# Norm weights and identity loaded on ACT's queue, and 18 matmuls on a zeroed tile ahead of the first input

## The chip, the core and the metric

The kernel runs on one core of a Trainium2 chip. The core has five engines that run side by side: TensorE (PE, matrix multiply), VectorE (DVE), ScalarE (ACT), GpSimd (POOL) and SyncE (SP). SP, ACT and POOL can issue DMA transfers. The metric is the device time of one execution in microseconds, median of several.

## The reference

One inference step of a two-layer encoder for 1024 prompt frames and 8 x 16 sample frames, that is 1152 tokens of width 1024 in all, in float32. Cut to what matters here, layer 0 begins so:

```python
xn = _rmsnorm(x, norm_g)                    # x * rsqrt(mean(x*x) + 1e-6) * norm_g
z = jnp.einsum('btd,de->bte', xn, w_in)     # 1024 -> 3584 columns
q, k, v, g_a, u_b, v_b, g_b = jnp.split(z, L0_SPLITS, axis=-1)
```

Differential attention and a spatial gate follow, an output projection, then layer 1 (a convolution module), and a last norm. The change touches only the first norm's weights `norm_g`, the identity matrix that the transposes use, and what PE does before its first input.

## The kernel before, in words

The 1152 tokens are 9 tiles of 128. For each tile `phase_qkv` loads `x` (128 x 1024, 512 KB), normalises it (`norm_transpose`), transposes it on PE in 8 blocks of 128 x 128 (`transpose_split`) and splits the result into a high part `xh` (a cast on ACT, L167) and a low part `xl` (a subtraction on DVE, L168). Matrix products are made of three products of such halves (`mm3`, L155): high by high, high by low, low by high. The weights are split the same way by `split_w`: a chunk `raw` of 512 KB is loaded by SP (L137), cast to `wh` on ACT (L143), and the remainder `wl` made on DVE (L144). One weight block of 512 columns has four such chunks, and each chunk serves two of the eight steps of a product. Three `raw` buffers exist, so the fourth chunk is loaded once the first has been split. `x` has two buffers, so tile 2 is loaded once tile 0 has been normalised.

Tile 0 is normalised in halves (`norm_out`): two sums of squares on ACT (L187), their sum on DVE (L188), a scale and offset (L123), a power on POOL (L124, `rr`), and two multiplications by `rr` and the norm weights `gb` on DVE (L193). `gb` holds `norm_g` in all 128 partitions, which one broadcast DMA fills (L114). The first product after that is the value projection, 24 matmuls of 512 columns per token tile, then keys and queries.

Each engine works through its own list in order. Those lists are written by a scheduler that reorders what the source says, so an edit at the top can change the order of casts on ACT and DVE. DMAs issued by one engine are queued in the order of issue.

## Time and profile before

| | us |
|---|---|
| median of 3 runs | 1261.32 |
| lowest and highest of these | 1260.91, 1264.07 |
| the profiled execution's own time | 1257.52 |
| its span, first to last instruction | 1255.7 |
| PE busy in the span | 1186.4 (94%) |
| PE's share of the chain that ended last | 77% |

PE is busy through nearly all of the span, so what counts is when its stream of work starts in earnest and where it stops. The table's PE time is no measure of PE's speed: matmuls overlap, and at the lower of the two clocks that the trace shows each one takes longer. In the timeline each row is a start, a duration, an engine, a line of the kernel, the operation, and in brackets how long the engine sat idle before it and what released it. In the chain of waits each row is a start, a duration and what held the end at that moment.

### The profile page before, as it was taken

How to read it: one execution, taken by the hardware profiler on the slowest of the kernel's cores; microseconds unless marked ns; L12 is line 12 of the kernel's file. 1: busy time of each engine (PE TensorE's matmuls, PEld its weight loads, DVE VectorE, ACT ScalarE, POOL GpSimd, SP SyncE). 2: the span in 40 equal slices, each digit the busy share in tenths (PEclk: the TensorE clock that was granted, in tenths of full speed). 3: DMA queues.
4: the chain of work that ended last, by engine and by line, in shares of the span. 5: the costliest groups of instructions: out<-in, count | busy, mean ns of one | idle time of the engine just before them, and what ended most of it. 6: DMA issues, size and time to landing. Idle time of an engine off the chain costs nothing.

```text
span 1255.7 us, 18564 instructions
## 1 busy us (share of the span) xinstructions
PE 1186.4 (94%) x6644; PEld 1078.1 (86%) x6644; DVE 830.0 (66%) x1695; ACT 477.6 (38%) x1090; POOL 365.6 (29%) x540
## 2 busy tenths in 40 slices
PE   6999999999989997889999999999999987999997
PEld 5878998999989887778888878999999987997886
DVE  5420225788687878686666535799999999267843
ACT  4431223445454545574544434211121212156421
POOL 2223223435353426222222221211424220033200
PEclk9999999999989999899999999999999997999999
DMA  8352444414141315685666545213231310212222
GB/s 295 106 164 70 152 150 128 119 55 116 39 124 42 112 41 163 225 287 203 223 213 232 185 150 184 66 40 88 72 108 49 122 59 24 67 35 101 101 96 73
DMA packets 121924, 153.26 MB, mean 122 GB/s; under 512 B 13577, under 2 KB 85281, under 8 KB 121824
## 3 DMA queue, kind: packets, MB, share of 16 engines
q1 hardware_dynamic: 107848, 108.21, 27.9%
q0 software_dynamic: 13840, 43.60, 10.2%
q8 instruction: 53, 0.87, 0.3%
q14 instruction: 39, 0.32, 0.1%
q10 hardware_dynamic: 144, 0.26, 0.1%
HBM read 116.22 MB, written 36.26 MB: 121 GB/s over the span
## 4 chain that ended last, share of the span: by engine, by line
PE 77%; DMA 8%; DVE 6%; ACT 4%; issue 2%; POOL 2%; SPq 0%; DVEq 0%; POOLq 0%; ACTq 0%
PE mm L155 50%; PE out L155 8%; PE py L1175 3%; PE S L155 3%; PE pa L589 2%; PE tr L416 2%; DMA vraw<-in_cache_v 2%; PE tr L165 2%; PE S L546 1%; PE S L547 1%; PE mm L787 1%; PE mm L761 1%; PE mm L786 1%; PE tr L584 1%; DVE wl L144 1%
## 5 line engine op out<-in xcount | busy, mean ns | idle before, releaser
L155 PE MATMUL mm<-yh,wh 128*128 128x384 f32 x576 | 196.5, 341 | 15.1 <-ACT sg L1024 12.6
L155 PE MATMUL mm<-yl,wh 128*128 128x384 f32 x576 | 195.2, 339 | 0.0
L155 PE MATMUL mm<-yh,wl 128*128 128x384 f32 x576 | 194.8, 339 | 0.0
L155 PE MATMUL mm<-wh,xh 128*128 128x384 f32 (+1 forms) x504 | 185.4, 369 | 1.3 <-DVE sg L469 0.6
L155 PE MATMUL mm<-wl,xh 128*128 128x384 f32 (+1 forms) x504 | 184.3, 366 | 1.7 <-DVE wl L144 1.7
L1151 DVE SCALAR_TENSOR_TENSOR acc<-u,cc,acc 128x1024 f32<-128x1024 f32 x145 | 185.4, 1279 | 0.4
L155 PE MATMUL mm<-wh,xl 128*128 128x384 f32 (+1 forms) x504 | 183.5, 364 | 0.0
L144 DVE TENSOR_TENSOR wl<-raw,wh 128x1024 fp32r<-128x1024 f32 (+1 forms) x72 | 91.3, 1274 | 91.6 <-ACT wh L143 91.0
L155 PEld LDWEIGHTS mm<-yh,wh 128*128 128x128 f32 x576 | 109.0, 189 | 15.9 <-ACT sg L1024 12.9
L155 PEld LDWEIGHTS mm<-yl,wh 128*128 128x128 f32 x576 | 109.1, 189 | 0.3
L155 PEld LDWEIGHTS mm<-yh,wl 128*128 128x128 f32 x576 | 109.0, 189 | 0.1
L155 PEld LDWEIGHTS mm<-wh,xh 128*128 128x128 f32 x504 | 95.5, 190 | 12.6 <-issue 1.1
L155 PEld LDWEIGHTS mm<-wl,xh 128*128 128x128 f32 x504 | 95.7, 190 | 11.7 <-DVE wl L144 3.2
L155 PEld LDWEIGHTS mm<-wh,xl 128*128 128x128 f32 x504 | 95.5, 190 | 8.8 <-DVE xl L168 0.3
L143 ACT CAST wh<-raw 128x1024 fp32r<-128x1024 f32 (+1 forms) x72 | 71.6, 1003 | 68.3 <-PE mm L155 30.6
L124 POOL TENSOR_TENSOR rr<-pw,mhalf 128x1 f32<-128x1 f32 x59 | 34.6, 586 | 169.2 <-DVE pw L123 160.8
L560 ACT ACTIVATE e<-S,nm 128x512 f32<-128x512 f32 (+5 forms) x96 | 55.2, 579 | 49.8 <-DVE nm L555 34.5
L1169 POOL TENSOR_TENSOR tw<-wx,same 128x640 f32<-128x640 f32 x24 | 37.4, 1560 | 80.3 <-PE py L1175 70.9
L552 DVE TENSOR_REDUCE nm<-S 128x1 f32<-128x512 f32 (+5 forms) x96 | 52.4, 550 | 12.1 <-PE S L547 11.4
L155 PE MATMUL out<-wh,cl 128*128 128x512 f32 x144 | 59.7, 415 | 0.0
L155 PE MATMUL out<-wh,ch 128*128 128x512 f32 x144 | 57.7, 401 | 1.7 <-DVE xr L847 1.2
L155 PE MATMUL mm<-wl,ch 128*128 128x512 f32 x144 | 56.9, 395 | 2.3 <-DVE wl L144 2.2
(287 smaller groups left out, 2572.7 us busy)
## 6 DMA issues: line engine op xcount, KB each, us to landing
raw<-in_cache_k SPq DMA_DIRECT2D x32, 512.0 KB, 4.5
vraw<-in_cache_v POOLq DMA_DIRECT2D x32, 512.0 KB, 5.2
raw<-in_w_in SPq DMA_DIRECT2D x24, 512.0 KB, 5.1
raw<-in_w_out SPq DMA_DIRECT2D x16, 512.0 KB, 4.1
raw<-in_w_in SPq DMA_DIRECT2D x32, 256.0 KB, 3.6
raw<-in_w_in SPq DMA_DIRECT2D x48, 128.0 KB, 3.2
s_y<-xr POOLq DMA_DIRECT2D x9, 512.0 KB, 5.5
x<-s_y SPq DMA_DIRECT2D x9, 512.0 KB, 4.1
```

What stands on the lines that cost most here:

```text
L124: m = nc.gpsimd.tensor_tensor(out, v[:, :w], self.mhalf[:, :w], ALU.pow)
L143: nc.scalar.copy(h[:, :ks * n], raw[:, :ks * n])
L144: (low or nc.vector).tensor_tensor(l[:, :ks * n], raw[:, :ks * n], h[:, :ks * n].bitcast(F32), ALU.subtract)
L155: m = self.nc.tensor.matmul(out, lhsT=x, rhs=y, start=(i == 0), stop=(i == n - 1))
L165: nc.tensor.transpose(ps[:, k * P:(k + 1) * P], src[:, kk * P:(kk + 1) * P], self.ident)
L416: nc.tensor.transpose(ps[:, h * P:(h + 1) * P], src[:, h * P:(h + 1) * P], self.ident)
L552: nc.vector.tensor_reduce(nm[:, j:j + 1], s[:, :n], AX.X, ALU.max, negate=True)
L560: nc.scalar.activation(e[:, j * n:(j + 1) * n], S[j][:, :n], AF.Exp, bias=nv, accum_out=zz[:, j:j + 1])
L589: nc.tensor.matmul(po, lhsT=wT[:, k * P:(k + 1) * P], rhs=hd["v"][:, k, :], start=(k == 0), stop=(k == qb))
L1151: tap = nc.vector.scalar_tensor_tensor(cv[:, :T] if k == CONV - 1 else acc, u[:, k:k + T], w1, acc, ALU.mult, ALU.add)
L1169: nc.gpsimd.tensor_tensor(tw.rearrange("p s (c f) -> p s c f", f=8), wx[:, g, :].rearrange("p (s f) -> p s f", f=8).unsqueeze(2).broadcast ...
L1175: nc.tensor.matmul(py, lhsT=tw[:, 4 - s, :], rhs=X[:, g, s:s + 176], start=(s == 0), stop=(s == 4))
```

## The change

Before the first token tile is loaded, a tile `warm` of 128 x 384 is zeroed on DVE, and PE multiplies two 128 x 128 pieces of it 18 times into a buffer that nothing reads. `gb` is loaded in two halves of 512 columns (256 KB each) from ACT's queue instead of in one piece from SP's, and the identity also goes to ACT's queue. `warm` takes a turn in the rotation of the `qh` buffers and the product a turn of the `pg` buffers.

```diff
+WARM = 18
...
+            warm = wk.tile([P, 384], F32, name="qh")
+            nc.vector.memset(warm, 0.0)
+            pw_ = pg.tile([P, 512], F32, name="pg")
+            for i in range(WARM):
+                nc.tensor.matmul(pw_[:, i % 4 * P:(i % 4 + 1) * P], lhsT=warm[:, :P], rhs=warm[:, P:2 * P], start=True, stop=True)
+            g0 = a["norm_g0"].partition_broadcast(P)
             for t in range(NT):
                 x = self.stage.tile([P, D], F32, name="x")
                 if t == 0:
                     for i in range(2):
                         nc.sync.dma_start(out=x[:, i * 512:(i + 1) * 512], in_=self.xrow(t)[:, i * 512:(i + 1) * 512])
+                        nc.scalar.dma_start(out=self.gb[:, i * 512:(i + 1) * 512], in_=g0[:, i * 512:(i + 1) * 512])
                 else:
                     nc.sync.dma_start(out=x, in_=self.xrow(t))
                 if t == 0:
-                    self.bcast(self.gb, a["norm_g0"])
-                    nc.sync.dma_start(out=self.ident, in_=a["cst"][:, :P])
+                    nc.scalar.dma_start(out=self.ident, in_=a["cst"][:, :P])
                 self.norm_transpose(x, self.gb, t)
```

The scheduler moves some casts. ACT's list at the start of the program before the change (`xs` with `x` alone is a sum of squares, `cst_58` the identity):

```order
L187 ACT_TABLE_LOAD
L187 ACTIVATE xs,ss_118<-x 128x512 x2
L143 CAST wh<-raw 128x1024
L167 CAST xh_82<-tr 128x4x128
L167 CAST xh_83<-tr 128x4x128
L143 CAST wh<-raw 128x1024 x2
L173 ACTIVATE xs,ss<-x 128x1024 x2
```

and ACT's list there with the change, where line numbers below the new constant are higher by one:

```order
L379 DMA gb<-in_norm_g 128x512 x2
L383 DMA cst_58<-in_cst 128x128
L188 ACT_TABLE_LOAD
L188 ACTIVATE xs,ss_140<-x 128x512 x2
L144 CAST wh<-raw 128x1024 x2
L168 CAST xh_82<-tr 128x4x128
L144 CAST wh<-raw 128x1024
L168 CAST xh_83<-tr 128x4x128
L174 ACTIVATE xs,ss<-x 128x1024 x2
```

Three DMA issues now stand ahead of everything on ACT, and the cast of the second weight chunk stands ahead of the first cast of the transposed tile. DVE's list at the same place before the change:

```order
L193 SCALAR_TENSOR_TENSOR xs<-x,rr,gb 128x512 x2
L144 TENSOR_TENSOR wl<-raw,wh 128x1024
L168 TENSOR_TENSOR xl_84<-tr,xh_82 128x4x128
L168 TENSOR_TENSOR xl_85<-tr,xh_83 128x4x128
L144 TENSOR_TENSOR wl<-raw,wh 128x1024 x2
```

and with the change:

```order
L194 SCALAR_TENSOR_TENSOR xs<-x,rr,gb 128x512 x2
L145 TENSOR_TENSOR wl<-raw,wh 128x1024 x2
L169 TENSOR_TENSOR xl_84<-tr,xh_82 128x4x128
L145 TENSOR_TENSOR wl<-raw,wh 128x1024
L169 TENSOR_TENSOR xl_85<-tr,xh_83 128x4x128
```

The remainder of the second weight chunk now stands ahead of the first low part of the tile. PE's list gains the 18 matmuls at its head and is otherwise in the same order; SP's loses the two loads. Behind these places the lists of all engines hold the same instructions in the same order.

## The prediction

> **What bounds the kernel now.** I read the chain of waits first, because PE is busy 94% of the span and the question is only when its unbroken stream begins. The rows are start, duration and what held the end (pieces left out are marked):

> ```profile
> 1.65 6.50 DMA gb<-in_norm_g
> ...
> 8.27 1.43 DVE xs L193 x2
> ...
> 9.77 7.33 DMA x<-in_x_prompt
> ...
> 17.18 1.16 ACT xs L173 x2
> ...
> 20.38 1.23 DVE wl L144
> ...
> 21.65 1.43 PE mm L155 x5
> ...
> 94.82 82.47 PE mm L155 x429
> ```

> The first 21.65 us hang on two transfers: the norm weights, landed at 1.65 + 6.50 = 8.15, and token tile 2, issued once tile 0 is normalised and landed at 17.10. Then ACT squares tile 2, casts the fourth weight chunk, and DVE makes that chunk's remainder. PE resumes at 21.65. The busy time by stretch shows that it does not stop again before 177:

> ```profile
> 22.00:60.00 38.00, 38.00 (x192) 31.47 (x191) 18.41 (x33) 16.86 (x31) 11.34 (x21) 1.00 0.55 161
> 60.00:177.00 117.00, 117.00 (x593) 103.40 (x592) 20.68 (x26) 28.05 (x45) 32.58 (x53) 1.00 0.37 120
> ```

> PE's busy time is the first figure after the comma, the clock the third last. So whatever the change does is worth what it moves 21.65; everything behind follows PE and shifts with it. The timeline of the start says who was late for whom:

> ```profile
> 0.73 1.28 ACT L187 ACT_TABLE_LOAD   x1 [0.73 <-PEq L1201]
> 3.33 0.63 ACT L187 ACTIVATE xs<-x 128x512 f32<-128x512 f32 x1 [1.31 <-DMA x<-in_x_prompt]
> 3.98 0.63 ACT L187 ACTIVATE xs<-x 128x512 f32<-128x512 f32 x1
> 5.16 0.55 POOL L124 TENSOR_TENSOR rr<-pw,mhalf 128x1 f32<-128x1 f32 x1 [4.72 <-DVE pw L123]
> 8.27 1.41 DVE L193 SCALAR_TENSOR_TENSOR xs<-x,rr,gb 128x512 f32<-128x512 f32 x2 [3.19 <-DMA gb<-in_norm_g]
> 9.08 1.97 PE L165 MATMUL tr<-cst,xs 128*128 128x128 f32 x8 [9.08 <-DVE xs L193]
> 9.73 1.05 ACT L143 CAST wh<-raw 128x1024 fp32r<-128x1024 f32 x1 [5.04 <-DMA raw<-in_w_in]
> 11.32 0.79 PE L155 MATMUL mm<-wh,xh 128*128 128x512 f32 x1 [0.27 <-ACT xh L167]
> 13.29 0.63 PE L155 MATMUL mm<-wh,xh 128*128 128x512 f32 x1
> 13.71 0.63 PE L155 MATMUL mm<-wl,xh 128*128 128x512 f32 x1
> 17.22 0.39 PE L155 MATMUL mm<-wh,xl 128*128 128x512 f32 x1
> 17.45 0.39 PE L155 MATMUL mm<-wh,xh 128*128 128x512 f32 x1
> 18.13 1.04 PE L165 MATMUL tr<-cst,xs 128*128 128x128 f32 x8
> 18.44 1.05 ACT L143 CAST wh<-raw 128x1024 fp32r<-128x1024 f32 x1
> 21.65 0.50 PE L155 MATMUL mm<-wl,xh 128*128 128x512 f32 x1 [0.89 <-DVE wl L144]
> ```

> Two things stand here. `rr` is ready at 5.71 and DVE waits 2.5 us longer for the weights. And PE runs at half speed at first: matmuls start 0.42 us apart at 13.29 and 0.23 us apart at 17.22, though the granted clock reads 1.00 throughout these stretches. From 13.29 to about 16.3 PE thus spends some 3 us on 1.5 us of work.

> **The load on ACT's queue.** ACT's last store shows what one issue costs there:

> ```profile
> 1252.74 0.37 ACTq L195 DMA_DIRECT2D out_y_sample<-yo  x1
> ```

> Three issues are 1.1 us, ahead of the table load of 1.28 us. They end at 0.73 + 1.1 + 1.28 = 3.1, and the first square starts at 3.33 with 1.31 us of waiting before it, so they cost nothing while `x` lands no earlier than that. SP saves two issues, but its weight loads stand behind `x` and would not land sooner for it.

> What can be won is in the transfers. By stretch (last two figures: share of the DMA engines, GB/s):

> ```profile
> 3.50:4.50 1.00, 0.00 (x0) 0.00 (x0) 0.00 (x0) 1.00 (x3) 0.00 (x0) 1.00 1.59 233
> 4.50:5.50 1.00, 0.00 (x0) 0.00 (x0) 0.31 (x2) 0.20 (x2) 0.34 (x1) 1.00 0.35 83
> 5.50:8.50 3.00, 0.00 (x0) 0.00 (x0) 0.23 (x1) 0.00 (x0) 0.21 (x1) 1.00 0.89 312
> 15.50:19.00 3.50, 3.50 (x19) 2.87 (x17) 1.50 (x4) 1.71 (x3) 0.95 (x2) 1.00 0.99 341
> ```

> While the broadcast runs, from about 3.5 to 5.5, the rate falls to 233 and 83 GB/s. Against 312 that is (1 - 233/312) + (1 - 83/312) = 0.25 + 0.73 = 1.0 us lost. With the broadcast in halves and between the packets of `x`, fewer of its reads meet at a time; that this recovers the loss is my assumption. The bounds: at best the weights are there when `rr` is, and 8.27 becomes 5.75, a gain of 2.5. At worst `x` and `gb` share the engines evenly and both land when `gb` does now, at 8.15. From the second square's start at 3.98 to the end of `rr` at 5.71 is 1.73 us, so DVE would start at 8.15 + 1.73 = 9.9, a loss of 1.6. I take +1.0 as the value, since the transfers behind (weights, tile 2, the fourth chunk) are moved at a nearly full share, 0.99 from 15.5 to 19, and gain what the queue gains, no more.

> [...]

> **The 18 matmuls.** A float32 128 x 128 product shows as two records each: the four matmuls at L279 appear as eight.

> ```profile
> L279 PE MATMUL pg<-x 32*128 32x384 f32 x8 | 3.4, 520 | 0.0
> 260.87 1.50 PE L589 MATMUL pa<-vnh,wT 128*128 128x128 f32 x12
> 422.36 1.97 PE L589 MATMUL pa<-vnh,wT 128*128 128x128 f32 x8
> L979 DVE MEMSET ones<- 128x128 f32 x1 | 0.2, 165 | 0.1
> ```

> At full speed six products start within some 1.3 us (the next instruction starts at 262.13), 0.21 us each; at half speed four take 1.6 to 2.0 us, 0.4 each. Zeroing 128 x 384 is at most three times 0.165, so PE starts at about 1.3. All 18 slow are 7.2 us, all fast 3.8 us: they end between 5.1 and 8.5. The transposes can't start before 6.5 (5.75 and one multiplication), so at worst they are 2 us late, and even then end about when they end now (9.08 + 1.97), because at full speed they take 1.04. On the path to 21.65 the matmuls cost nothing: PE's cover is the wait for weights until 9.73.

> Their worth depends on whether speed lasts until the products start, and on PE being late at all. PE reached tile 1's transposes at 18.13 and finished them at 19.2, 2.5 us before the chunk that held it at 21.65. About 1.5 us saved on PE there is hidden by that chunk; it counts only as far as the chunk comes earlier too, by the 1.0 above. And the trace shows how little idling is enough to lose the speed:

> ```profile
> 419.10:422.50 3.40, 1.91 (x12) 1.18 (x11) 3.28 (x10) 1.62 (x6) 0.00 (x0) 1.00 0.37 101
> 422.50:425.90 3.40, 3.40 (x16) 3.40 (x17) 2.11 (x6) 1.18 (x5) 0.67 (x1) 0.50 0.51 157
> ```

> After 3.4 us with PE busy for 1.91, the clock was 0.50. Between the end of the 18 matmuls and the first products near 11 to 13 us PE has only about 1 us of transposes, less than that. I expect the speed lost again in most executions.

> [...]

> **The moved casts.** `xh` now stands behind the second chunk's cast on ACT. That chunk's landing is bounded by the two single loads:

> ```profile
> 2.59 1.64 SPq L137 DMA_DIRECT2D raw<-in_w_in  x3
> raw<-in_w_in SPq DMA_DIRECT2D x1, 512.0 KB, 7.1
> raw<-in_w_in SPq DMA_DIRECT2D x2, 512.0 KB, 8.4
> 12.69 0.80 PE L155 MATMUL mm<-wh,xl 128*128 128x512 f32 x1
> ```

> The first lands at 9.7; the second and third, issued near 3.1 and 3.7, take 8.4 in the median, so the second lands near 11.2. At the old landings its cast ends at 12.25, `xh` at 12.8, the second remainder on DVE (1.22) at 13.5 and `xl` at 14.2 where it was 12.6. PE's third product starts 1.5 us later, and 16 products follow up to the transposes: at 0.2275 they end at 17.8, before today's 18.13; at 0.425 at 21.0. This reorder costs nothing while PE is fast from about 17 on, which one busy window of 3.4 us from 14 gives.

> **The sum.** Profiled time 1257.5, minus 1.0 for the transfers, minus 0 for PE, plus 0 for issues and casts: 1256.5. The median shown lies 3.8 above the profiled time, so I carry the difference over: 1261.3 - 1.0 = 1260.3.

> **Rivals.**
> (a) Hidden anyway: `x` delayed by as much as `gb` gains. For it: total bytes are unchanged and the share is near full. Time 1261.3.
> (b) Slower: the cast order with the clock lost. PE's third product at 14.2, all 16 slow to 21.0, eight transposes at 1.97 to 23.0, where they ended at 19.2; three products stood between them and 21.65 with waits, about 1.0 us at the slow rate, so 24.0 in place of 22 or so: +2.0, 1263.3. It decides once the eight transposes of tile 1 end later than 20.7. Against it: one busy window ends the slow stretch.
> (c) More: the weights meet `rr` and the clock holds, 2.5 us, 1258.8. For it: the 2.5 us that DVE waits; against it: what lands behind still shares the engines.

> **Chances.** Forecast 0.45, (a) 0.25, (b) 0.15, (c) 0.15. All four lie within 3.8 us, 0.3% of the time, below which a measurement of this kernel can't be told from no change; its three runs alone spread over 3.2 us. So no change 0.88; faster by more 0.08, for (c) with a lucky pair of medians; slower by more 0.04, for (b) likewise. The runs lie up to 2.7 us from their median, and a median of several moves less: the range takes 2 us below (c), 1256.8, and 1 us above (b), 1264.3, which is the less likely of the two ends to be passed.

> **What would show it.** The sum of squares starting near 3.3 shows ACT's issues hidden, and later shows `x` delayed. `xs` at L194 before 8.27 shows the load part right. Matmul starts 0.42 us apart after 11 us show the speed lost. The restart of PE's unbroken stream against 21.65 is the whole effect; if it moves and the time does not move by as much, a wait behind 177 took it back. A gain over 4 us would mean that the start was bounded by something I took for cover.

## The result: slower, and not where the change is made

The changed kernel takes 1268.08 us in the median of six runs (1263.97 to 1270.63), against 1260.62 for the kernel before beside it (1257.45 to 1264.07). The ratio is 1.0059, with a 95% interval of 1.0036 to 1.0083: slower, by some 7 us, outside the range given. One execution of a kernel below, the profiled one of `h2_from762`, ran almost wholly at half the clock (1980 us) and is left out everywhere.

The start went much as the prediction's parts said, though not for all of its reasons. The timeline of the changed kernel (start, duration, engine, line, instruction, and in brackets the idle time before it and what ended it; lines behind the edit are 7 higher than before, the helpers ahead of it 1):

```profile
0.74 0.89 ACTq L379 DMA_DIRECT2D gb<-in_norm_g  x2
1.35 5.84 PE L372 MATMUL pg<-qh 128*128 128x128 f32 x36 [1.35 <-DVE qh L369]
2.14 1.28 ACT L188 ACT_TABLE_LOAD   x1 [2.14 <-issue]
5.98 0.63 ACT L188 ACTIVATE xs<-x 128x512 f32<-128x512 f32 x1 [2.55 <-DMA x<-in_x_prompt]
8.40 0.55 POOL L125 TENSOR_TENSOR rr<-pw,mhalf 128x1 f32<-128x1 f32 x1 [7.96 <-DVE pw L124]
8.98 1.41 DVE L194 SCALAR_TENSOR_TENSOR xs<-x,rr,gb 128x512 f32<-128x512 f32 x2 [0.66 <-POOL rr L125]
9.79 1.32 PE L166 MATMUL tr<-cst,xs 128*128 128x128 f32 x8 [2.60 <-DVE xs L194]
13.55 0.79 PE L156 MATMUL mm<-wh,xl 128*128 128x512 f32 x1 [0.15 <-DVE xl L169]
14.14 0.63 PE L156 MATMUL mm<-wh,xh 128*128 128x512 f32 x1
14.56 0.63 PE L156 MATMUL mm<-wl,xh 128*128 128x512 f32 x1
19.50 1.03 PE L166 MATMUL tr<-cst,xs 128*128 128x128 f32 x8
```

The norm weights no longer end a wait: DVE's multiplication at 8.98 now waits for `rr`. But `rr` is 3.2 us later than before (8.40 against 5.16), because the first half of `x` lands later, as its square shows: 5.98 against 3.33. The 18 products end at 7.19. At 14.14 matmuls start 0.42 us apart, so PE is at half speed again. The stretches of 3.41 us around it (PE's busy time is the figure behind the comma, the clock the third last) show when it was lost:

```profile
4.64:8.06 3.42, 2.55 (x23) 2.36 (x21) 0.09 (x1) 1.45 (x4) 0.00 (x0) 1.00 1.02 383
8.06:11.47 3.41, 1.31 (x8) 0.84 (x8) 2.71 (x5) 1.93 (x2) 0.55 (x1) 1.00 1.30 506
11.47:14.88 3.41, 2.56 (x5) 1.64 (x6) 3.30 (x5) 3.13 (x6) 0.00 (x0) 0.50 0.71 252
```

After a stretch with PE busy for 1.31 us the clock is 0.50, and stays so until 18.29.

The chain of waits of the changed kernel (start, duration, what) shows what bounds the start now, and what happened later:

```profile
10.59 1.05 ACT wh L144
...
13.55 6.11 PE mm L156 x16
19.66 0.87 PE tr L166 x8
...
20.77 1.89 PE mm L156 x7
...
94.43 82.47 PE mm L156 x429
...
198.88 3.54 DMA s_ga<-big
...
204.93 5.36 DMA s_ga<-big
...
211.12 3.02 PE mm L156 x12
214.14 0.12 PE S L553
```

From 13.55 to 176.90 PE has no wait, with the 16 products, most of them at half speed, now on the chain; the product that began at 21.65 begins at 21.34. The same run of 429 products starts at 94.43 where it started at 94.82, so this execution is 0.39 us ahead, and still is at 177. That is no more than executions differ by: in three kernels below that leave the start as it was (`g4_mid18`, `h1_from558`, `i3_from762_again`) the product of 21.65 begins at 20.97, 20.99 and 21.11, and the run of 429 at 94.18, 94.16 and 94.27. Behind 177 the changed kernel falls back. Near 200 PE runs without a wait in the kernel before, whose chain has there:

```profile
205.49 7.30 PE mm L155 x32
212.79 0.12 PE S L546
```

In the changed kernel two stores of the gate (`s_ga`) take 3.54 and 5.36 us, PE waits, and the score product that began at 212.79 begins at 214.14. At the end the profiled execution is 6.5 us behind (1263.97 against 1257.52), in steps that all lie behind 177: none of it is at the place of the change.

### The profile page after: what moved, and what is told of

The parts are those of the page before. It is cut to its first block, busy times and chain, and to the rows that moved or that the text cites. A ratio compares the mean times of both kernels' runs of the same rounds, so it can differ in the third digit from the quotient of the medians.

```text
span 1262.2 us, 18639 instructions
## 1 busy us (share of the span) xinstructions
PE 1191.7 (94%) x6680; PEld 1083.7 (86%) x6680; DVE 830.2 (66%) x1696; ACT 476.9 (38%) x1090; POOL 364.1 (29%) x540
## 3 DMA queue, kind: packets, MB, share of 16 engines
q0 software_dynamic: 13840, 43.60, 10.1%
## 4 chain that ended last, share of the span: by engine, by line
PE 73%; DVE 10%; DMA 8%; ACT 4%; issue 3%; POOL 2%; SPq 0%; DVEq 0%; POOLq 0%; ACTq 0%
PE mm L156 48%; PE out L156 7%; DVE acc L1158 3%; PE S L156 3%; PE pa L596 2%; DMA raw<-in_w_in 2%; PE py L1182 2%; PE tr L423 2%; DMA vraw<-in_cache_v 1%; PE tr L166 1%; PE S L553 1%; PE S L554 1%; DVE wl L145 1%; PE mm L794 1%; DMA s_ga<-big 1%
## 5 line engine op out<-in xcount | busy, mean ns | idle before, releaser
L156 PE MATMUL mm<-yh,wh 128*128 128x384 f32 x576 | 196.9, 342 | 15.1 <-ACT sg L1031 12.6
L145 DVE TENSOR_TENSOR wl<-raw,wh 128x1024 fp32r<-128x1024 f32 (+1 forms) x72 | 90.4, 1262 | 91.7 <-ACT wh L144 90.9
L156 PEld LDWEIGHTS mm<-yh,wh 128*128 128x128 f32 x576 | 109.4, 190 | 15.9 <-ACT sg L1031 12.8
L144 ACT CAST wh<-raw 128x1024 fp32r<-128x1024 f32 (+1 forms) x72 | 71.7, 1002 | 65.2 <-PE mm L156 30.6
L567 ACT ACTIVATE e<-S,nm 128x512 f32<-128x512 f32 (+5 forms) x96 | 55.1, 578 | 50.7 <-DVE nm L562 36.7
## 6 DMA issues: line engine op xcount, KB each, us to landing
raw<-in_cache_k SPq DMA_DIRECT2D x32, 512.0 KB, 4.5
vraw<-in_cache_v POOLq DMA_DIRECT2D x32, 512.0 KB, 5.6
raw<-in_w_in SPq DMA_DIRECT2D x24, 512.0 KB, 5.1
raw<-in_w_out SPq DMA_DIRECT2D x16, 512.0 KB, 3.9
s_y<-xr POOLq DMA_DIRECT2D x9, 512.0 KB, 5.5
x<-s_y SPq DMA_DIRECT2D x9, 512.0 KB, 4.4
```

Source lines behind the costliest of these rows:

```text
L144: nc.scalar.copy(h[:, :ks * n], raw[:, :ks * n])
L145: (low or nc.vector).tensor_tensor(l[:, :ks * n], raw[:, :ks * n], h[:, :ks * n].bitcast(F32), ALU.subtract)
L156: m = self.nc.tensor.matmul(out, lhsT=x, rhs=y, start=(i == 0), stop=(i == n - 1))
L567: nc.scalar.activation(e[:, j * n:(j + 1) * n], S[j][:, :n], AF.Exp, bias=nv, accum_out=zz[:, j:j + 1])
```

## The experiments

Each run is timed beside runs of the kernel before on the same chip; the ratios are to those. The small products were put where they leave the order of all other instructions on each engine as it was in the kernel before; in the kernels with 64 wide products one cast (and the remainder made from it), and in the two with 46 products behind the head a few neighbours, change places.

### Which part of the change

Four kernels were run first: the products alone; the loads alone (`gb` in one piece); the whole change with the zeroed tile in other memory; and the kernel before with one more DMA.

```diff
 e1_warm_only: the kernel before, and
+            warm = wk.tile([P, 384], F32, name="qh")
+            nc.vector.memset(warm, 0.0)
+            (the 18 products)
 e2_loads_only: the kernel before, and
-                    self.bcast(self.gb, a["norm_g0"])
-                    nc.sync.dma_start(out=self.ident, in_=a["cst"][:, :P])
+                    nc.scalar.dma_start(out=self.gb, in_=a["norm_g0"].partition_broadcast(P))
+                    nc.scalar.dma_start(out=self.ident, in_=a["cst"][:, :P])
 e3_own_buffer: the whole change, but
-            warm = wk.tile([P, 384], F32, name="qh")
+            warm = self.bd.rearrange("p h r -> p (h r)")[:, :384]
 e4_one_more_dma: the kernel before, but gb loaded in two halves on SP
```

> Only the 18 matmuls on a zeroed tile are added; the norm weights and the identity stay on SP's queue. The scheduler puts the second chunk's cast ahead of xh here too, and the rotation of the qh buffers moves by one, as in the changed kernel. If the matmuls or what comes with them (cast order, rotation) carry the loss: about 1268, 7 us over the kernel before. If the loads on ACT's queue carry it: 1260 to 1262. If any small shift of the start costs the same: 1266 to 1269.

> Only the loads move: norm weights (in one piece) and identity on ACT's queue, no matmuls, no rotation; only the cast of the second weight chunk changes places, as in the changed kernel. If the loads on ACT's queue carry the loss: 1266 to 1268. If the matmuls or the rotation carry it: 1260 to 1261. If any small shift of the start costs the same: 1266 to 1269.

> The changed kernel, with the zeroed tile in the memory of bd, which is filled only later, instead of in a turn of the qh buffers. So the waits of the first loads in the attention phase are those of the kernel before; loads, matmuls and cast order are those of the change. If the rotation of the buffers carries the loss: 1260 to 1262. If the loads, the matmuls or a mere shift carry it: 1266 to 1269.

> The kernel before, with the norm weights loaded in two halves on SP's queue: one more DMA, so that every later DMA signals on the next semaphore in turn, as in the changed kernel; no matmuls, no ACT queue, the same order on every engine. If the turn of the semaphores or any small shift of the start carries the loss: 1266 to 1269. Otherwise 1260 to 1262.

Measured: the products alone 1265.06, ratio 1.0042 [1.0020, 1.0065]; the loads alone 1261.18, 1.0005 [0.9986, 1.0023]; the tile in other memory 1266.09, 1.0042 [1.0019, 1.0066]; one more DMA 1262.57, 1.0012 [0.9989, 1.0035]; the kernel before 1260.77.

The products carry the loss. The cast that changes places is not the cause, since it does so with the loads alone too, nor is the buffer that the products take from the rotation of `qh`, since the loss stays without it; one more DMA shows no loss either, though its interval reaches 1.0035. The loads alone move PE's restart from 21.65 to 20.33 us in their trace (20.97 to 21.11 in the three others with the old start), and the time does not show it.

### What the products leave behind them

What could 18 products at 1 to 7 us do to the work at 200 us and later? The profile lists, beside the program's own DMA queues, q8, which it names instruction. The first lines and the queue's line of the kernel before (queue, packets, MB, share):

```profile
span 1255.7 us, 18564 instructions
...
PE 1186.4 (94%) x6644; PEld 1078.1 (86%) x6644; DVE 830.0 (66%) x1695; ACT 477.6 (38%) x1090; POOL 365.6 (29%) x540
...
q8 instruction: 53, 0.87, 0.3%
```

53 packets of 16.4 KB, one about every 23 us. PE has 13,288 matmuls and weight loads in these records, 251 per packet; with the 262 semaphore waits and drains that the trace has of PE besides, it is 13,550, or 255.7. My estimate from these counts is 256 in a packet. If these packets bring PE's instructions, then 18 float32 products, which are 36 matmuls and 36 weight loads, bring each later packet 72 instructions earlier against the work, some 6 to 7 us (72 of 256 in 23 us), and other transfers meet it. I call this the fetch theory. By it the size of the products does not matter, only their count, and a count of 64 products, 256 instructions, puts every packet back to where it was. The rival is that the products count as PE work.

```diff
 f1_tiny18: the kernel before, with warm and its memset as in the change, and
+            for i in range(18):
+                nc.tensor.matmul(pw_[:1, i % 4 * P:i % 4 * P + 1], lhsT=warm[:, :1], rhs=warm[:, P:P + 1], start=True, stop=True)
 f2_tiny64: range(64)       f4_tiny36: range(36)
 f3_wide64: the same with 64 products of
+                nc.tensor.matmul(pw_[:32, i % 4 * P:i % 4 * P + 40], lhsT=warm[:, :32], rhs=warm[:, P:P + 40], start=True, stop=True)
```

> The kernel before with 18 float32 products of the zeroed tile that are 1 x 1 in place of 128 x 128: the same 72 PE instructions (two matmuls and two weight loads each), next to no PE time, no moved casts. Theory F (instruction fetch): the queue of instruction fetches brings one 16 KB packet per 256 PE instructions, and 72 more instructions at the head bring every later fetch some 6 us earlier against the program, onto transfers that the path waits for. F expects the loss in full, 1265 (1263.5 to 1267, ratio 1.002 to 1.005), and fetches 5 to 8 us earlier against the work around 200 and 900. Theory C: the loss comes from what the 18 full products do as work (PE busy for 6 us early, another clock history). C expects 1260.6, ratio 0.999 to 1.001.

> The same with 64 products of 1 x 1: 256 PE instructions, one whole fetch packet. F expects the fetches to stand against the work where they stood before, one number later, and so the old time, 1260.6 (ratio 0.999 to 1.0015). C, if it is the early PE activity that counts, expects at least what the 18 small ones cost, and up to 1265, since 128 small matmuls keep PE busy some 5 us.

> 64 products of 32 x 40 in place of the 18 of 128 x 128: about the same PE time (2560 columns against 2304) and the same moved casts, but 256 PE instructions. F expects the old time, 1260.6 or up to 0.5 less (ratio 0.998 to 1.0015). C expects the loss in full, 1265 to 1266 (ratio 1.003 to 1.006).

> 36 products of 1 x 1, 144 PE instructions, a little over half a packet. F expects a time of its own that follows from which transfers the fetches now meet: anything from 1257 to 1267, and not what C says unless by chance. C expects 1260.6, as for the 18 small ones (ratio 0.999 to 1.001).

Measured, against 1261.00: 18 small products 1267.22, ratio 1.0055 [1.0031, 1.0080]; 64 small 1259.82, 0.9995 [0.9980, 1.0009]; 64 wide 1260.46, 1.0006 [0.9988, 1.0024]; 36 small 1259.97, 0.9995 [0.9978, 1.0012].

Eighteen products of one element, 1.04 us of PE in a time when PE has nothing to do, cost the whole loss. Sixty-four wide ones that keep PE busy for 6.4 us cost nothing, and neither do sixty-four small ones, 3.34 us of PE where some 5 were expected. The rival falls. The first lines of the kernel with 64 small products show one packet more, for 256 PE instructions and one memset:

```profile
span 1259.9 us, 18821 instructions
...
q8 instruction: 54, 0.88, 0.3%
```

The packets' starts in the traces, in us, near the head and near 600:

```
before      31.6   55.1   87.5  109.7 ...  603.2  623.5  648.1
18 small    25.8   46.8   74.0  100.0 ...  603.3  623.5  641.2
64 small     8.1   29.9   54.3   82.3  108.7 ...  605.6  626.5  650.7
```

With 64 there is one at 8.1, and the later ones stand about where they stood, apart from 1 to 3 us by which executions run earlier or later, and 5 us once (82.3 against 87.5; in `h1_from558`, which is the kernel before up to there, it is at 82.8). With 18 they stand near 600 where they stood, but that execution comes to the work there later: the value tile shown below is issued at 617.99 and not at 614.63.

That these packets are PE's can be counted in the traces. In all 19 at the usual clock the n-th packet starts when PE has started at least 151 + 256 (n - 1) instructions (matmuls, weight loads, semaphore waits and drains, the added ones included), and in the median of each trace 161 to 175 + 256 (n - 1). So a packet belongs to 256 PE instructions, and its place follows from their count. That PE itself has to wait for its instructions shows nowhere: behind 22 us it has a single wait that is put down to nothing in the profile, of 2.9 us before, 3.0 with the change and 2.9 with 18 small products.

A count of 82 should then be as slow as 18, and the whole change with 64 products as fast as before.

```diff
 g1_after64: the whole change, with the 64 products of 32 x 40 in place of the 18
 g2_tiny82: the kernel before, with 82 products of 1 x 1 at the head
```

> The whole change, with 64 products of 32 x 40 in place of the 18 of 128 x 128: the loads on ACT's queue, the moved casts and some 6 us of early PE work stay, and 256 PE instructions are added in place of 72. Theory F (the fetches of PE instructions meet other transfers) expects the loss gone: 1260.5 (1259 to 1262, ratio 0.998 to 1.002). If the loss belonged to the loads and the full products together, it stays at 1266 to 1268 (ratio 1.004 to 1.007).

> The kernel before with 82 products of 1 x 1, 328 PE instructions: one whole packet more than the 18 small products that cost 6 us. F expects the loss of those back: 1266 (1264 to 1268, ratio 1.003 to 1.006), with the fetches where they stood with 18. If 18 small products were slow for another reason than the place of the fetches, 82, like 36 and 64, show 1260.5 (ratio 0.998 to 1.001).

Measured, against 1260.86: 1261.17, ratio 1.0007 [0.9988, 1.0027], and 1266.09, 1.0044 [1.0022, 1.0065]. Both as the fetch theory had it. The first holds the loads, the moved casts and the early PE work of the change, and loses nothing; so the change's 7 us go with the count of PE instructions, and with it with the place of the fetches.

### Where it is lost

Two kernels move the fetches in one stretch only.

```diff
 g3_head_and_mid: 18 products of 1 x 1 at the head, and in values()
+                for i in range(46 if (h, qb) == (3, 0) else 0):
+                    nc.tensor.matmul(po[:1, :1], lhsT=self.ident[:, :1], rhs=self.ident[:, :1], start=True, stop=True)
 g4_mid18: none at the head, and in gm_piece()
+                for i in range(18 if (g, t) == (1, 0) else 0):
+                    nc.tensor.matmul(ps[:1, :1], lhsT=self.ident[:, :1], rhs=self.ident[:, :1], start=True, stop=True)
```

> 18 products of 1 x 1 at the head and 46 more in the values of the last head's first query tile (its last in order, near 515 us): 72 PE instructions ahead of that place, 256 behind it, so that only the fetches from 7 to some 515 us are moved. F, with the loss mainly at the stores of the gate near 200 us (some 2 us there in three of four slow traces) expects 1263 (1261.5 to 1265). With the loss behind 515 us, 1261 to 1262, of which up to 1.2 are the 46 products themselves. If the place of the fetches did nothing, the time of the 18 alone stays, 1266 to 1268.

> The kernel before with 18 products of 1 x 1 ahead of the first product of the second gate group (near 335 us) and none at the head: only the fetches behind 335 us are moved, by 72 instructions; the products themselves take some 0.5 to 1 us of PE there. F, with the loss mainly near 200 us expects 1262.5 to 1264; with the loss behind 335, 1265 to 1267.

Measured: moved from 7 to 515 us 1261.38, ratio 1.0011 [0.9996, 1.0026]; moved from 335 us on 1267.16, 1.0064 [1.0041, 1.0087]. The first expectation named the stores near 200, from the traces; that was wrong. They are slow in some executions, but what PE loses there does not reach the end. Most of the loss, at the least, is made behind 515: the interval of the first reaches 3.3 us, of which its 46 products may be up to 1.2.

One place there is the same in every trace. The decode stage loads tiles of the value cache (`vraw`), and ACT casts them when they land. The timeline of the kernel before, and then of the changed one:

```profile
614.63 0.73 POOL L775 DMA_DIRECT2D vraw<-in_cache_v  x1 [0.47 <-DVE vl L779]
621.63 1.05 ACT L778 CAST vh<-vraw 128x1024 fp32r<-128x1024 f32 x1 [1.69 <-DMA vraw<-in_cache_v]
```

```profile
616.65 0.73 POOL L782 DMA_DIRECT2D vraw<-in_cache_v  x1 [0.47 <-DVE vl L786]
625.36 1.05 ACT L785 CAST vh<-vraw 128x1024 fp32r<-128x1024 f32 x1 [3.38 <-DMA vraw<-in_cache_v]
...
629.55 0.63 PE L423 MATMUL tr<-cst,raw 128*128 128x128 f32 x4 [0.94 <-PE out L156]
```

From issue to cast it is 7.00 us before and 8.71 after; ACT waits 1.69 and 3.38, and PE waits behind ACT. In that stretch (614.6 to 621.6) the queues of the kernel before hold no packet of instructions, and the tiles issued in it, this one and the next, take 6.7 us from issue to landing:

```profile
q0 software_dynamic: 377, 1.41, 49.8%
q1 hardware_dynamic: 402, 0.99, 45.5%
vraw<-in_cache_v POOLq DMA_DIRECT2D x2, 512.0 KB, 6.7
```

In the changed kernel (616.6 to 625.3) one lies in it, at 622.2, and the tiles take 8.5:

```profile
q1 hardware_dynamic: 579, 1.37, 48.8%
q0 software_dynamic: 427, 1.56, 44.7%
q8 instruction: 1, 0.02, 0.7%
vraw<-in_cache_v POOLq DMA_DIRECT2D x2, 512.0 KB, 8.5
```

Over the traces of all kernels at the usual clock: the eight with a packet between issue and cast (the changed kernel, the products alone, the tile in other memory, 18 and 82 small, moved from 335, from 558, and up to 762) wait 2.87 to 3.38 us for the tile. The eleven others wait 1.38 to 2.19. No trace lies between. PE then sits idle for 0.43 to 0.94 us in the eight and not at all in the others, but has part of it back by 660. So a fetch that falls into a transfer on the path makes it later by some 1.2 us (the medians of the waits are 3.1 and 1.9): that much is shown. It is a small part of the loss.

Three kernels cut behind 515 further, by the same means.

```diff
 h1_from558: 18 products of 1 x 1 in main() where (t, i) == (0, 0)
 h2_from762: 18 in main() where (t, i) == (8, 0)
 h3_head_762: 18 at the head, 46 in main() where (t, i) == (8, 0)
 the products are
+                    nc.tensor.matmul(ps[:1, :1], lhsT=self.ident[:, :1], rhs=self.ident[:, :1], start=True, stop=True)
```

> The kernel before with 18 products of 1 x 1 ahead of the first product of the decode stage's output projection (558 us): the fetches are moved by 72 PE instructions only behind 558 us. If the loss sits behind 558 (the cache value load near 620 and what follows), it comes back in full, 1266 (1264 to 1268, ratio 1.003 to 1.006), and the trace waits 3.0 us or more for the value tile near 620 where the kernel before waits 1.7. If the loss sits between 335 and 558, 1261 to 1262.

> The same with the 18 small products ahead of token tile 8's output projection (near 762 us): only the fetches behind 762 us are moved. If the loss is at the value load near 620 and in what follows from its 1 us, 1261 to 1262 (ratio 1.000 to 1.001, up to 1 us for the products). If fetches meet transfers of the convolution stage behind 762, 1264 to 1267 (ratio 1.003 to 1.005).

> 18 products of 1 x 1 at the head and 46 more ahead of token tile 8's output projection, 256 in all behind it: the fetches are moved from 7 to 762 us and stand as before behind that. The complement of the run before: 1265 to 1267 if the loss comes from ahead of 762 (the 46 themselves cost up to 1.2 of it), 1261 to 1262.5 if it comes from behind.

Measured, against 1260.13: from 558 on 1264.64, ratio 1.0031 [1.0013, 1.0050]; from 762 on 1266.13, 1.0042 [1.0024, 1.0060]; up to 762 alone 1264.86, 1.0034 [1.0015, 1.0053]. The value tile of the first waits 3.13 us, as expected. But the two complements cost 6.0 and 4.7 us, where either the one or the other was to be free, and both together, as 18 at the head, 6.2. By the medians the loss does not add up over places. By the intervals it may: they are 3.0 to 7.6 us, 1.9 to 6.7 and, for both together, 3.9 to 10.1, so that some 3 us from either side of 762 would fit them all.

It could still have been the 18 products at 762 that stall the work by standing there. The last three put the fetches behind them back without taking them away.

```diff
 i1_head46_762: 46 products of 1 x 1 at the head, and 18 in main() where (t, i) == (8, 0)
 i2_head46: the 46 at the head alone
 i3_from762_again: as h2_from762
```

> 46 products of 1 x 1 at the head and 18 ahead of token tile 8's output projection (near 762 us), 256 PE instructions in all: the same 18 at the same place as in the run that cost 6 us, but the fetches behind them stand as in the kernel before; ahead of them they are moved by 184. If the fetches behind 762 carry the loss: 1261 to 1262 plus what 184 costs ahead of 762 (not known; 0 to 4). If the 18 products stall the conv stage by their place: 1266 or more.

> 46 products of 1 x 1 at the head alone, 184 PE instructions, all fetches moved by 184 (72 short of a full turn). No theory gives its time beforehand; it says what 184 cost, so that the run with the products at 762 can be read: 1258 to 1267.

> The kernel with 18 small products at 762 once more, for a trace at the usual clock: 1266 (1264 to 1268) again. If fetches do it, the trace waits near 200 and near 620 us as the kernel before does, and loses its time behind 762, in longer waits of PE or in more time at the half clock.

Measured, against 1260.96: 1258.10, ratio 0.9982 [0.9961, 1.0003]; 1258.19, 0.9984 [0.9962, 1.0006]; 1263.59, 1.0024 [0.9999, 1.0048]. With the 46 at the head the 18 at 762 cost nothing (1258.10 against 1258.19), so their place is not it. What stays open is why fetches moved by 184 cost nothing anywhere, where 72 do. The repeat is slower by 2.6 us, not by 6; the intervals of the two overlap, and its direction is the same only just (some 3 us would fit both). Its trace waits 1.92 us for the value tile, as foretold, since its fetches are moved only behind it. 184 instructions give the quickest times of the study, 2.8 us under the kernel before, though the intervals just reach 1.

### What goes with the loss

The slower of these kernels spend more time at half the clock. The table has the mean granted clock over the timed executions, and the time at half clock worked out from it as 2 x (1 - clock) x span, since the records know only 1.0 and 0.5. Kernels with full or wide products are left out: their start has half-clock stretches of its own.

| kernel | median, us | clock | at half clock, us |
|---|---|---|---|
| before, four sets | 1260.1 to 1261.0 | 0.9795 to 0.9803 | 49.6 to 51.7 |
| 18 small | 1267.2 | 0.9746 | 64.4 |
| 82 small | 1266.1 | 0.9772 | 57.8 |
| from 335 | 1267.2 | 0.9769 | 58.6 |
| from 762 | 1266.1 | 0.9769 | 58.4 |
| up to 762 | 1264.9 | 0.9767 | 59.0 |
| from 558 | 1264.6 | 0.9776 | 56.6 |
| from 762, again | 1263.6 | 0.9785 | 54.3 |
| 7 to 515 | 1261.4 | 0.9802 | 49.8 |
| 36 small | 1260.0 | 0.9802 | 49.9 |
| loads alone | 1261.2 | 0.9796 | 51.4 |
| one more DMA | 1262.6 | 0.9786 | 54.0 |
| 64 small | 1259.8 | 0.9807 | 48.6 |
| 46 at the head | 1258.2 | 0.9804 | 49.2 |
| 46 and 18 | 1258.1 | 0.9817 | 45.9 |

In the changed kernel matmuls of 512 columns start some 0.42 us apart at half clock, up to 18.29, and some 0.23 apart behind it, so a microsecond at half clock costs PE about half a microsecond of work: from 335 on, 8.0 us more of it would be 4.0 of the 6.3 lost; for 46 and 18, 5.8 less would be 2.9 of 2.9 gained. The 46 alone do not follow this: they gain 2.8 with 2.5 us less, which would be 1.2. Nor does the pair of traces at the start. These are the rows from 22 us to the end, of the kernel before and of the changed one (length of the stretch, then PE's busy time):

```profile
22.00:1255.70 1233.70, 1175.03 (x6607) 1070.10 (x6605) 819.17 (x1680) 466.68 (x1073) 360.87 (x529) 0.98 0.38 119
```

```profile
22.00:1262.20 1240.20, 1174.86 (x6605) 1070.07 (x6603) 818.19 (x1679) 465.81 (x1073) 358.55 (x527) 0.98 0.38 118
```

PE is busy for the same time in both, and the 6.5 us between them are all waits of PE (1233.70 - 1175.03 = 58.7 against 65.3). In the trace of the 18 small products it is the other way round: PE waits for 60.6 and is busy for 1184.90, 9.9 more. So the loss shows as waits in one execution and as half clock in another. The stretches show one place where the clock differs. These are the rows from 790 to 800 of the kernel before, of the changed one, and of the one with 18 small products (clock third last):

```profile
790.00:800.00 10.00, 10.00 (x60) 9.93 (x59) 5.76 (x16) 1.25 (x3) 3.01 (x2) 1.00 0.04 12
```

```profile
790.00:800.00 10.00, 7.79 (x36) 7.71 (x37) 3.27 (x8) 2.88 (x5) 4.56 (x3) 0.83 0.19 39
```

```profile
790.00:800.00 10.00, 7.42 (x29) 7.18 (x30) 1.85 (x3) 3.23 (x5) 4.78 (x6) 0.66 0.27 57
```

PE comes there out of waits for the norm of the last tiles (0.7 us before, 1.7 with the change, 1.4 with 18 small products, between 770 and 800); in the kernel before it resumes at full speed, in the two others at half speed, for 3.4 and 6.8 us. One trace of each proves nothing; what there is lies in the table's means. That a late transfer lengthens a wait of PE until the clock falls, and that this is how fetches of a microsecond become 5 us, fits the slower kernels of the table, but not the first pair of traces. It was not shown: no run held the clock while the fetches moved. It is also open which transfers behind 558 are the ones met, beside the value tile.

## Why the prediction was wrong, by its steps

**What bounds it.** The chain to 21.65 was read rightly, and PE's stream does not stop before 177 in the changed kernel either. The step that failed is the sentence drawn from it: "whatever the change does is worth what it moves 21.65; everything behind follows PE and shifts with it". The 0.39 us by which the changed kernel's trace is ahead stood until 177 and were worth nothing, and they are no more than executions of the old start differ by: the same 72 instructions that were costed at no time moved the fetches against what lies behind, and the time grew by 7 us. The 64 products are the counter-test: with the whole start of the change the time is the old one.

**The load on ACT's queue.** The issues are hidden, as said: the first square waits 2.55 us for `x` behind the table load. The transfers, sized at +1.0, gave the loads alone, with `gb` in one piece, 1.3 at the restart (21.65 to 20.33), or 0.6 to 0.8 against the other traces with the old start, so the size was near, but by luck, for the way was another: `xs` at L194 did not come before 8.27 but at 8.98. That is the case of the lower bound, `x` and `gb` sharing the engines, at nearly half of its price (8.27, 8.98, 9.9): in the first 8 us of the changed kernel SP's queue takes 42.5% of the engines' time and the one with the new loads 24.0%, and the first square of `x` starts at 5.98 and not at 3.33. What came sooner were the weight chunks behind: with the loads alone the first is cast at 8.56, against 9.73 before. None of it can be told in the time (ratio 1.0005 [0.9986, 1.0023]). That halves of `gb` recover what the broadcast loses was an assumption, and no run shows it.

**The 18 matmuls.** They run from 1.35 to 7.19, inside the 5.1 to 8.5 given for their end, and the speed was lost again, as expected: the stretch before the loss had PE busy for 1.31 of 3.41 us. One busy stretch ended the loss, as the prediction had it: from 14.88 to 18.29 PE is busy throughout at 0.50, and to 21.70 the clock is 1.00 again; so it is in the kernel before, where the stretch behind the busy one of 422.50 to 425.90 reads 1.00. "Minus 0 for PE" left out a cost that some executions have: with the 16 products at half speed on the chain this one gains 0.39 where the loads alone gain 1.4 by then, a term of 1.0 us. Its half clock lasts 6.83 us; in the trace of the tile in other memory, whose start has the same work, it lasts 3.41 us from 12.39, the run of 429 starts at 93.59, and the term is gone. That was rival (b)'s place; the transposes of tile 1 end at 20.53, just short of its 20.7.

**The moved casts.** The third product starts at 13.55, 0.86 us later in place of 1.5, and the eight transposes begin at 19.50, between the 17.8 and 21.0 of the two rates.

**The rivals and the chances.** All four cases placed the change's worth at the start and lay within 3.8 us of the old time, and the 0.88 for no change rests on that alone. The prediction had the right sign of trouble in its last part, "a wait behind 177 took it back", but no case with a price for it: nothing in the sum asked what 72 more instructions on PE's list do to later work. The profile of the kernel before showed the queue that brings them, at 0.3% of the engines' time, and it was not read.

## What to carry to other kernels

Adding instructions to PE's list moved every later fetch of its instructions against the work (72 more put the second packet at 46.8 us in place of 55.1); in this kernel that alone was worth up to 6 us of 1261, and perhaps 3 us the other way, as much as many an edit is meant to bring. The other engines' lists were not tried. Before an edit is believed, or thrown away, run it with padding that changes the number of instructions and nothing else (here tiny products on an idle PE, up to one packet of 256): if the time moves with the padding, the edit's own worth is the part that doesn't. An instruction that costs no time where it stands may still have a price elsewhere: here 1.04 us of products on an idle PE, and 6.2 us at the end.
